# Two RWKV chunks in step, precedence for their short operations, and later rotary sums, in a two-layer hybrid block

## The chip, the cores and the metric

The kernel runs on one core of a Trainium2 chip. The metric is the device time of one execution in microseconds; the median of several runs is compared. The profile is of one further execution. TensorE, the engine of the matmuls, appears in it as PE, its weight loads as PEld; VectorE is DVE, ScalarE is ACT, GpSimd is POOL, and SyncE, which issues nearly all DMA transfers, is SP.

## The reference

Two layers over 256 context tokens and 1024 latent tokens of width 1024. Each layer normalises and modulates, projects once, and gives the columns to three groups of heads: gated linear attention (GLA), windowed softmax attention with rotary positions, and RWKV-7. Their outputs go through one output projection, and a SwiGLU feed-forward part follows. The change is about the RWKV group, whose recurrence is this one, in two directions, for 4 heads of 64:

```python
def step(S, inp):
    rt, wt, kt, vt, kkt, at = inp
    sa = jnp.einsum('bhvk,bhk->bhv', S, kkt)
    S = (S * wt[:, :, None, :] - sa[..., None] * (kkt * at)[:, :, None, :]
         + vt[..., None] * kt[:, :, None, :])
    return S, jnp.einsum('bhvk,bhk->bhv', S, rt)
```

and about the rotary positions of the latent queries and keys, `x1*cos - x2*sin` and `x1*sin + x2*cos`.

## The kernel before

A layer runs in stages: the RWKV input columns (`in_rwkv`), the *mixer stage* (`mixers`, line 771), the windowed attention together with the backward GLA states, GLA with the output projection, the feed-forward part. The change touches the mixer stage of both layers, the first norms of the kernel, and one cost.

**How work is ordered.** On TensorE the order is written out by hand. `Weave` (line 721) holds generators ("jobs"). A job issues matmuls, and with them the operations of other engines, then yields how many nanoseconds later its next matmuls are due, or a condition (`after`, on keys such as `("s", i)`, "scan i is done") that must be known first. `TE.t` is the planner's clock: each matmul adds a cost (lines 154 to 160). `run` picks the job that is due first, the lowest rank on a tie. Rank 9 is the *filler*, `dense()`: the projections of 12 columns of 128 for the two other groups (`in_rest`), matmul by matmul, and a thirteenth column after the scan. Whenever the filler had less than 1000 ns of the last 3400, it is picked (`SHARE`, lines 24 and 749). The RWKV jobs start 22 or 20 us of planned time after the filler (`LEAD`). On the other engines, SP's DMA queue included, a scheduler decides at compile time: among operations whose inputs it takes to be there it issues the one that was traced first, and each engine then runs its queue strictly in that order, waiting at the head where an input is late.

**RWKV in the mixer stage** (`rwkv_mixer`, line 1104). 1280 tokens are 20 chunks of 64; chunk i is taken for both directions and all heads at once, as 4 pairs `u`. To solve a chunk's triangular system a unit lower matrix is inverted by doubling. `prep_a` (line 1168) loads the chunk (`load`, two DMA issues of `AK`), makes the Gram product `LQ` (16 records `ps_g`, evicted and masked by DVE in `gram`), takes the 2x2 level from a copy `ld`, and does levels 2 and 3. `prep_b` (line 1193) loads `VU` and `Vbd` (six DMA issues), scales `Ke` on POOL, does level 4, the Gram product `MP`, level 5, a sixth level of 64x64 blocks (`ps_y6`, `ps_w6`, written into `XF`), and transposes `Ke` into `KT`. A `level` (line 1143) is a chain of four links: 16 matmuls of 32x32 into `ps_y`, ACT's copy to `y` (line 1148), 1000 ns later 16 matmuls into `ps_w`, DVE's predicated copy into `X` (line 1153) and its block transpose into `XT` (line 1154), 1200 ns later the next level. A float32 matmul shows as two records in the profile. `scan` (line 1248) carries the state `SBD` through the chunks: `R` from `MP`, `Vbd` and the state (evicted to `Rbd` by DVE and ACT), then `X` times `R`, `VU`/`U`, the state update `ps_s`, and the outputs. `finish` (line 1294) normalises the outputs of a token block with some two dozen short DVE operations. Ranks: scan 0, `prep_b` 1, `prep_a` 2, `finish` 3; `prep_a` may be three chunks ahead of the scan, `prep_b` two.

**Drains of the filler** (`drain`, line 611, rank -1). ACT copies a finished `ps_in` bank (two banks of tag d). For queries and keys of latent tokens the halves are exchanged by four DMA transfers into `t1`; DVE multiplies `t1` by the sine (line 643), POOL multiplies `y` by the cosine (line 644), DVE adds (line 645). `in_gla` (line 674, rank -2) makes GLA's decays for 256 tokens, each direction ending with transposes through `tokens_of`; its `ps_gl` and the transposes share one PSUM bank (tag x).

**The start** (lines 1710 to 1732): the squares and their sums of the three token groups (`norm.add`) are issued first, then the norms of the three groups (`start_in`), then the first columns.

Of the kernel before, what the change touches and what calls it, by code (L numbers as in the profile page):

```python
# [10 lines left out]
F32 = mybir.dt.float32  # L11
# [134 lines left out]
def block_kernel(ctx: ExitStack, tc: tile.TileContext, a):  # L146
# [3 lines left out]
    class Tensor:  # L150
# [3 lines left out]
        def matmul(self, out, lhsT, rhs, **kw):  # L154
            n, k, m = math.prod(rhs.shape[1:]), lhsT.shape[0], math.prod(lhsT.shape[1:])
            if rhs.dtype == F32:
                self.t += n * 1.06 if k <= 32 else max(130.0 if m <= 64 else 215.0, n * 1.67)
            else:
                self.t += n / 2.4
            return nc.tensor.matmul(out, lhsT, rhs, **kw)  # L160
# [5 lines left out]
    TE = Tensor()  # L166

# [435 lines left out]
    def in_rest(l, h, cols, wpool, pool, own, ypool, pp, spawn):  # L603
# [7 lines left out]
        def drain(nm, g0, n, ps):  # L611
# [13 lines left out]
            elif nm[:2] == "gg":  # L625
                j = int(nm[2])
                th = tmp("th")
                S.activation(th[:, :n], y[:, :n], AF.Tanh, scale=0.5)
                V.scalar_tensor_tensor(y[:, :n], th[:, :n], 1.0, y[:, :n], ALU.add, ALU.mult)
                V.tensor_scalar(y[:, :n], y[:, :n], hc(l, "glan"), None, ALU.mult)  # L630
                SY.dma_start(d_gg[:, j, g0:g0 + n], y[:, :n])
            elif nm == "sv":
                yield 1300
                tokens_of(aux, tmp, y, g0, n, d_sv)
            else:
                if g0 >= CTX:
                    r0 = g0 - CTX
                    rp = ypool.tile([P, 2, 512], F32, name="rope", bufs=1)
                    SY.dma_start(rp, a["rope"][:, :, r0:r0 + 512])
                    t1 = tmp("t1")  # L640
                    for r in range(0, P, 32):
                        SY.dma_start(t1[r:r + 32], y[r ^ 32:(r ^ 32) + 32])
                    V.tensor_tensor(t1, t1, rp[:, 1, :], ALU.mult)
                    G.tensor_tensor(y, y, rp[:, 0, :], ALU.mult)
                    V.tensor_tensor(y, y, t1, ALU.add)
                hl_ = [pool.tile([P, 512], F32R, name="qk_hl", tag="tmp", bufs=5) for _ in range(2)]
                S.copy(hl_[0][:, :n], y[:, :n])
                V.tensor_tensor(hl_[1][:, :n], y[:, :n], hl_[0][:, :n].bitcast(F32), ALU.subtract)
# [25 lines left out]
    def in_gla(l, t0, pool, own, pp, dw):  # L674
# [8 lines left out]
        for d in range(2):  # L683
# [21 lines left out]
            if not keys_only:  # L705
# [6 lines left out]
                      lambda name: pool.tile([P, 512], F32, name=name, tag="tmp", bufs=5), z, t0, n, d_gk[:, :, d, :])  # L712

# [390 lines left out]
    def rwkv_mixer(l, t_first, pool, fpool, pp, spawn):  # L1104
# [6 lines left out]
        lev = pool.tile([P, 5, 128], U8, name="lev")  # L1111
        for i in range(5):
# [3 lines left out]
            V.tensor_copy(lev[:, i, :], lf.rearrange("p d n -> p (d n)"))  # L1116
# [16 lines left out]
        def gram(AK, w_, dst):  # L1133
            ps = new([P, 4, P], "ps_g")
# [7 lines left out]

        def level(lv, LQ, X, XT):
            py = new([P, 4, 32], "ps_y")
            for u, rs, cs in blocks:
                TE.matmul(py[rs, u, :], LQ[rs, u, cs], XT[rs, u, :])
            y = pool.tile([P, 4, 32], F32, name="y", bufs=4)
            S.copy(y, py)
            yield 1000
            pz = new([P, 4, 32], "ps_w")  # L1150
            for u, rs, cs in blocks:
                TE.matmul(pz[rs, u, :], y[rs, u, :], X[rs, u, :])
            V.copy_predicated(f2(X), lev[:, lv - 1, :], f2(pz))
            V.transpose(f2(XT), f2(X))
            yield 1200
# [12 lines left out]
        def prep_a():  # L1168
            load(0)
            for i in range(NC):  # L1170
                yield after(("s", i - 3))
                b = batch[i]
                if i + 1 < NC:
                    load(i + 1)
                AK = b["AK"]
                X = pool.tile([P, 4, 32], F32, name="X", bufs=2)
                XT = pool.tile([P, 4, 32], F32, name="XT", bufs=2)
                G.tensor_copy(X, eye32.unsqueeze(1).to_broadcast([P, 4, 32]))
                LQ = pool.tile([P, 4, P], F32, name="LQ", bufs=3)
                gram(AK, 3, LQ)  # L1180

                ld = pool.tile([P, 4, 32], F32, name="ld")
                for r in range(0, 128, 32):
                    S.copy(ld[r:r + 32], LQ[r:r + 32, :, r % 64:r % 64 + 32])
                V.copy_predicated(f2(X), lev[:, 0, :], f2(ld))
                V.transpose(f2(XT), f2(X))
                yield 3400
                for lv in range(2, 4):
                    yield from level(lv, LQ, X, XT)
                b.update(LQ=LQ, X=X, XT=XT)  # L1190
                at["a", i] = TE.t + 900

        def prep_b():
            for i in range(NC):
                yield after(("a", i), ("s", i - 2))
                b = batch[i]
                cc, Dt, AK, LQ, X, XT = (b[n] for n in ("cc", "Dt", "AK", "LQ", "X", "XT"))
                VU = pool.tile([P, 512], F32, name="VU", bufs=3)
                vb = Vbd[i % 2]
                for d in range(2):  # L1200
                    c = cc[d]
                    src = d_v[c % 2 * 64:c % 2 * 64 + 64, c // 2, :]
                    SY.dma_start(VU[0:64, d * 256:(d + 1) * 256], src)
                    s4 = src.rearrange("s (q h n) -> s q h n", q=2, h=2)
                    for hp in range(2):
                        SY.dma_start(vb[H[hp], 2 * d:2 * d + 2, H[hp]], s4[:, :, hp, :])

                Ke = pool.tile([P, 4, P], F32, name="Ke")
                G.tensor_tensor(Ke, AK[:, :, 2:4, :].rearrange("p u w n -> p u (w n)"),
                                Dt.unsqueeze(2).to_broadcast([P, 4, P]), ALU.mult)  # L1210
                yield from level(4, LQ, X, XT)
                MP = pool.tile([P, 4, P], F32, name="MP", bufs=2)
                gram(AK, 2, MP)
                yield 0
                yield from level(5, LQ, X, XT)

                xf = XF[i % 2]
# [13 lines left out]
                KT = pool.tile([P, 4, P], F32, name="KT", bufs=2)  # L1231
# [11 lines left out]
                b.update(VU=VU, vb=vb, KT=KT, MP=MP, X=xf)  # L1243
                at["b", i] = TE.t + 900
# [3 lines left out]
        def scan():  # L1248
            for i in range(NC):
# [77 lines left out]
        for rank, gen in enumerate((scan(), prep_b(), prep_a(), finish_all())):  # L1327
            spawn(gen, rank, LEAD[l])
# [379 lines left out]
    with ExitStack() as e1:  # L1708
# [3 lines left out]
        with pool_of("x0", side="right") as xpool, pool_of("ad0", side="right") as apool, \  # L1712
# [198 lines left out]
```

## Time and profile before

| | us |
|---|---|
| median of 3 runs | 3771.24 |
| lowest and highest run | 3764.25, 3771.63 |
| the profiled execution | 3780.98 |
| its span, first to last instruction | 3779.2 |
| TensorE busy | 3598.1 (95%) |
| DVE, ACT, POOL busy | 2352.7, 1528.3, 692.3 |

A busy time is the union of an engine's instructions; matmuls overlap in the pipeline, so a busy TensorE isn't TensorE at its peak. The granted clock is a share of 2.4 GHz: 0.50 is the lower level, 1.2 GHz. "Idle before" an instruction is the time its engine stood still ahead of it, and the arrow names what ended that. "issue" is time for which the profile shows no wait.

### The profile page before, as it was taken

How to read it: one execution, taken by the hardware profiler on the slowest of the kernel's cores; microseconds unless marked ns; L12 is line 12 of the kernel's file. 1: busy time of each engine (PE TensorE's matmuls, PEld its weight loads, DVE VectorE, ACT ScalarE, POOL GpSimd, SP SyncE). 2: the span in 40 equal slices, each digit the busy share in tenths (PEclk: the TensorE clock that was granted, in tenths of full speed). 3: DMA queues.
4: the chain of work that ended last, by engine and by line, in shares of the span. 5: the costliest groups of instructions: out<-in, count | busy, mean ns of one | idle time of the engine just before them, and what ended most of it. 6: DMA issues, size and time to landing. Idle time of an engine off the chain costs nothing. (4 is left out here: it accounts for less than half of the span.)

```text
span 3779.2 us, 76437 instructions
## 1 busy us (share of the span) xinstructions
PE 3598.1 (95%) x30714; PEld 2823.4 (75%) x30714; DVE 2352.7 (62%) x4660; ACT 1528.3 (40%) x3170; POOL 692.3 (18%) x979
## 2 busy tenths in 40 slices
PE   7999999999999999999999998889999999999998
PEld 4767677656787888888888766667777778888787
DVE  4764545555567777756776783445566576666766
ACT  4444633345424333333442553543366243333213
POOL 3122222101234000000442232222211340000002
PEclk8999999999999999999999999989979999999999
DMA  5253342453231333325421234343321423221521
GB/s 181 104 171 107 110 126 85 116 162 92 88 109 63 113 112 106 116 70 196 134 91 57 86 146 124 112 122 112 87 81 35 129 101 97 77 89 62 195 67 62
DMA packets 310769, 405.79 MB, mean 107 GB/s; under 512 B 52880, under 2 KB 210192, under 8 KB 308368
## 3 DMA queue, kind: packets, MB, share of 16 engines
q1 hardware_dynamic: 310416, 400.92, 33.9%
q8 instruction: 242, 3.96, 0.4%
q14 instruction: 111, 0.91, 0.1%
HBM read 290.54 MB, written 105.03 MB: 105 GB/s over the span
## 5 line engine op out<-in xcount | busy, mean ns | idle before, releaser
L160 PE MATMUL ps_in<-h,w_hl 128*128 128x512 f32 (+1 forms) x2928 | 723.6, 387 | 12.3 <-ACT h L386 7.9
L160 PEld LDWEIGHTS ps_in<-h,w_hl 128*128 128x128 f32 x2928 | 491.0, 194 | 138.4 <-issue 50.1
L160 PE MATMUL ps_gu<-f,hl 128*128 128x512 f32 (+1 forms) x2400 | 568.6, 389 | 9.8 <-DVE hl L399 4.8
L160 PE MATMUL ps_d<-g,w_hl 128*128 128x512 f32 (+1 forms) x2688 | 557.4, 369 | 8.8 <-DVE x L1675 6.4
L160 PEld LDWEIGHTS ps_d<-g,w_hl 128*128 128x128 f32 x2688 | 463.8, 189 | 102.8 <-DVE x L1675 11.4
L160 PEld LDWEIGHTS ps_gu<-f,hl 128*128 128x128 f32 x2400 | 443.1, 190 | 105.2 <-DVE hl L399 5.7
L1675 DVE SCALAR_TENSOR_TENSOR x<-ps_d,mods,x 128x512 f32<-128x512 f32 (+1 forms) x448 | 291.0, 684 | 133.1 <-PE ps_d L160 132.4
L160 PE MATMUL ps_gu<-T,hl 128*128 128x512 f32 x1440 | 346.9, 390 | 1.5 <-DVE u L1576 1.5
L160 PEld LDWEIGHTS ps_gu<-T,hl 128*128 128x128 f32 x1440 | 268.8, 188 | 57.7 <-ACT g L398 1.9
L263 POOL TENSOR_TENSOR ada<-ada 128x256 f32<-128x256 f32 x112 | 90.5, 841 | 691.4 <-DMA x<-d_gt 560.0
L351 POOL TENSOR_TENSOR nacc<-nacc,nsq 128x512 f32<-128x512 f32 (+1 forms) x52 | 60.7, 1168 | 778.9 <-ACT nsq L350 776.2
L398 ACT CAST hl<-S 128x512 fp32r<-128x512 f32 x160 | 98.3, 621 | 252.4 <-PE ps_gu L160 159.1
L398 ACT CAST w_hl<-w_raw 128x1024 fp32r<-128x1024 f32 (+1 forms) x100 | 101.0, 1014 | 244.5 <-PE ps_d L160 194.1
L398 ACT CAST hl<-raw 128x512 fp32r<-128x512 f32 x156 | 96.6, 622 | 220.7 <-PE ps_gu L160 196.2
L1026 DVE TENSOR_REDUCE mx<-ps_ss 128x1 f32<-128x640 f32 (+2 forms) x144 | 107.5, 747 | 113.5 <-PE ps_ss L160 113.0
L160 PE MATMUL ps_o<-m,w_hl 128*128 128x512 f32 (+1 forms) x720 | 166.5, 381 | 0.0
L399 DVE TENSOR_TENSOR hl<-S,hl 128x512 fp32r<-128x512 f32 x160 | 109.9, 689 | 65.8 <-ACT hl L398 65.5
L160 PEld LDWEIGHTS ps_o<-m,w_hl 128*128 128x128 f32 x720 | 125.8, 191 | 32.5 <-issue 7.7
L399 DVE TENSOR_TENSOR w_hl<-w_raw,w_hl 128x1024 fp32r<-128x1024 f32 (+1 forms) x100 | 119.9, 1203 | 43.1 <-ACT w_hl L398 42.7
L399 DVE TENSOR_TENSOR pT<-ps_st,pT 128x512 fp32r<-128x512 f32 (+1 forms) x168 | 109.0, 657 | 33.8 <-ACT pT L398 33.4
L160 PEld LDWEIGHTS ps_x<-f,hl 128*128 128x128 f32 x960 | 124.5, 191 | 6.6 <-issue 0.8
L160 PE MATMUL ps_x<-f,hl 128*128 128x256 f32 x960 | 127.1, 283 | 0.0
(355 smaller groups left out, 6024.2 us busy)
## 6 DMA issues: line engine op xcount, KB each, us to landing
w_raw<-in_w_in_dram SPq DMA_DIRECT2D x44, 512.0 KB, 3.7
raw<-in_w_gate_dram SPq DMA_DIRECT2D x44, 512.0 KB, 3.7
raw<-in_w_up_dram SPq DMA_DIRECT2D x44, 512.0 KB, 3.5
x<-d_gt SPq DMA_DIRECT2D x88, 256.0 KB, 3.9
AK<-d_ab SPq DMA_DIRECT2D x80, 256.0 KB, 3.5
w_raw<-in_w_down_dram SPq DMA_DIRECT2D x40, 512.0 KB, 4.2
d_gt<-u SPq DMA_DIRECT2D x68, 256.0 KB, 2.0
d_ab<-W SPq DMA_DIRECT2D x16, 1024.0 KB, 4.2
```

The source lines that it names most:

```text
L160: return nc.tensor.matmul(out, lhsT, rhs, **kw)
L263: G.tensor_tensor(acc[:, s], acc[:, s], ps_[n % 2], ALU.add)
L351: (G if 0 < o < 5 else V).tensor_tensor(self.acc[g0], self.acc[g0], sq[:, :n], ALU.add)
L398: S.copy(dst[:, 0], src)
L399: V.tensor_tensor(dst[:, 1], src, dst[:, 0].bitcast(F32), ALU.subtract)
L1026: V.tensor_reduce(m_, psf[:, :nk * P], AX.X, ALU.max)
L1675: V.scalar_tensor_tensor(x[:, o, g0:g0 + n], ps[:, :n], mods[:, l, s, 40 + o:41 + o], x[:, o, g0:g0 + n], ALU.mult, ALU.add)
```

## The change

*Doublings in step.* `prep_a`, `prep_b` and `level` go. One job `prep` of rank 1 runs 21 iterations. Iteration i starts chunk i (the young one: load, `LQ`, 2x2 level) and ends chunk i - 1 (the old one: `VU`, `Vbd`, `Ke`, `MP` at the head of the iteration). Its two steps do levels 2 and 3 of the young chunk and levels 4 and 5 of the old one together: `X2` and `XT2` hold both chunks' matrices as two halves, one group of 32 matmuls fills `ps_y`, one copy of 256 columns evicts it, one group fills `ps_w`, one predicated copy and one transpose of 256 columns follow. The masks are laid out as `lev2` for either parity. The pauses stay 3400, 1000, 1200 and 300 ns. The sixth level, `XF` and `KT` follow for the old chunk.

*Precedence.* In `gram`, `prep` and `scan` the engines V, S and G are wrapped by `First`: each operation is traced under `tc.high_priority(600)`, that is, it counts for the scheduler as traced 600 instructions earlier. SP isn't wrapped.

*Rotary sums.* POOL's product with the cosine comes first and at once; the job then yields 3500 ns, and DVE's product with the sine is traced only then and pinned behind all that is traced on DVE up to that point (`keep_in_program_order`). The DVE sum and what follows are traced behind it.

*GLA.* Each direction of `in_gla` ends with a pause of 2000 ns.

*Planner's cost.* A float32 matmul with 64 rows and 64 columns of weights counts 0.9 ns a column.

*Start.* The squares and sums of the last token group are issued after the norms of the first two groups.

```diff
-                self.t += n * 1.06 if k <= 32 else max(130.0 if m <= 64 else 215.0, n * 1.67)
+                self.t += n * 1.06 if k <= 32 else n * 0.9 if k == m == 64 else max(130.0 if m <= 64 else 215.0, n * 1.67)
...
+    class First:
+        def __init__(self, engine):
+            self.engine = engine
+        def __getattr__(self, name):
+            def issue(*args, **kw):
+                with tc.high_priority(600):
+                    return getattr(self.engine, name)(*args, **kw)
+            return issue
+    FIRST = First(V), First(S), First(G)
...
-                    V.tensor_tensor(t1, t1, rp[:, 1, :], ALU.mult)
                     G.tensor_tensor(y, y, rp[:, 0, :], ALU.mult)
+                    yield 3500
+                    tc.keep_in_program_order(V.tensor_tensor(t1, t1, rp[:, 1, :], ALU.mult))
                     V.tensor_tensor(y, y, t1, ALU.add)
...
             tokens_of(lambda name: pp.tile([P, 512], F32, name=name, tag="x"),
                       lambda name: pool.tile([P, 512], F32, name=name, tag="tmp", bufs=5), z, t0, n, d_gk[:, :, d, :])
+            yield 2000
...
         def gram(AK, w_, dst):
+            V = FIRST[0]
...
+        X2 = pool.tile([P, 2, 4, 32], F32, name="X2")
+        XT2 = pool.tile([P, 2, 4, 32], F32, name="XT2")
...
-        def prep_a():
+        def prep():
+            V, S, G = FIRST
             load(0)
-            for i in range(NC):
+            for i in range(NC + 1):
                 yield after(("s", i - 3))
...
+                p = i % 2
+                young, old = batch[i] if i < NC else None, batch[i - 1] if i else None
+                hv = slice(0, 2) if i < NC and i else slice(p, p + 1) if old is None else slice(1 - p, 2 - p)
...
+                yield 3400 if young is not None else 0
+                both = [(h, b["LQ"]) for h, b in ((p, young), (1 - p, old)) if b is not None]
+                for step in range(2):
+                    py = new([P, 2, 4, 32], "ps_y")
+                    for h, LQ in both:
+                        for u, rs, cs in blocks:
+                            TE.matmul(py[rs, h, u, :], LQ[rs, u, cs], XT2[rs, h, u, :])
+                    y = pool.tile([P, 2, 4, 32], F32, name="y", bufs=2)
+                    S.copy(y[:, hv], py[:, hv])
+                    yield 1000
+                    pz = new([P, 2, 4, 32], "ps_w")
+                    for h, LQ in both:
+                        for u, rs, cs in blocks:
+                            TE.matmul(pz[rs, h, u, :], y[rs, h, u, :], X2[rs, h, u, :])
+                    V.copy_predicated(f3(X2[:, hv]), lev2[:, step, p, hv].rearrange("p h n -> p (h n)"), f3(pz[:, hv]))
+                    V.transpose(f3(XT2[:, hv]), f3(X2[:, hv]))
+                    yield 1200
...
         def scan():
+            V, S, G = FIRST
...
-        for rank, gen in enumerate((scan(), prep_b(), prep_a(), finish_all())):
+        for rank, gen in ((0, scan()), (1, prep()), (3, finish_all())):
...
-            for o in range(KD):
-                norm.add(o, *GROUPS[2])
             h = {}
-            for g0, n in GROUPS:
+            for i, (g0, n) in enumerate(GROUPS):
+                for o in range(KD if i == 2 else 0):
+                    norm.add(o, g0, n)
                 start_in(0, norm, act, h, g0, n)
```

## Rows read from the trace of the kernel before

**Rows 1.** the page of the profile: the whole execution
```profile
span 3779.2 us, 76437 instructions
```

**Rows 2.** windows of both mixer stretches: us, busy us by engine, clock, DMA
```profile
240.00:735.00 495.00, 457.68 (x8214) 357.01 (x8213) 237.16 (x741) 210.18 (x545) 115.65 (x208) 0.94 0.40 114
2262.00:2742.00 480.00, 431.01 (x8062) 330.04 (x8060) 229.68 (x684) 204.17 (x526) 118.31 (x211) 0.95 0.39 114
```

**Rows 3.** TensorE's waits, 240 to 735 us: who <- releaser: us, times, longest
```profile
PE ps_y L160 <- DVE XT L1154: 10.5, 11, 2.6
PE ps_g L160 <- DMA AK<-d_ab: 6.2, 1, 6.2
PE ps_gl L160 <- ACT vt L600: 4.3, 5, 1.7
PE ps_w L160 <- ACT y L1227: 3.5, 4, 1.4
```

**Rows 4.** TensorE's waits, 2275 to 2742 us
```profile
PE ps_r L160 <- ACT Rbd L1266: 12.6, 7, 4.3
PE ps_gl L160 <- ACT vt L600: 10.0, 5, 4.3
PE ps_y L160 <- DVE XT L1154: 8.0, 7, 4.2
PE ps_g L160 <- DMA AK<-d_ab: 6.5, 1, 6.5
```

**Rows 5.** timeline of 2505 to 2520 us: start, duration, instruction [idle before <-releaser]
```profile
2511.36 0.69 DVE L643 TENSOR_TENSOR t<-t,rope 128x512 f32<-128x512 f32 x1 [5.07 <-DMA t<-in]
2511.48 1.69 POOL L644 TENSOR_TENSOR in<-in,rope 128x512 f32<-128x512 f32 x1 [2.46 <-DMA t<-in]
...
2511.96 0.30 DVE L1153 COPY_PREDICATED X<-lev,ps_w 128x128 f32<-128x128 uint8 x1
...
2518.90 1.94 PE L160 MATMUL ps_r<-Rbd,XF 128*64 128x128 f32 x8 [4.31 <-ACT Rbd L1266]
```

**Rows 6.** windows of 4 us in layer 0's mixer stretch
```profile
344.00:348.00 4.00, 2.26 (x108) 1.94 (x109) 3.34 (x8) 3.41 (x6) 0.60 (x1) 0.99 0.30 66
348.00:352.00 4.00, 2.62 (x40) 2.15 (x40) 1.81 (x4) 1.45 (x5) 3.67 (x5) 0.50 0.60 201
```

**Rows 7.** windows of the tile ps_in alone, layer 1
```profile
2640.00:2660.00 20.00, 9.79 (x35) 1.00 0.42 124
2700.00:2720.00 20.00, 4.89 (x16) 1.00 0.20 56
```

**Rows 8.** timeline of 569 to 574 us: a lone group and a double one
```profile
569.40 0.34 PEld L160 LDWEIGHTS ps_y<-XT,LQ 32*32 32x32 f32 x32 [0.17 <-issue]
...
569.78 1.43 PE L160 MATMUL ps_in<-h,w_hl 128*128 128x512 f32 x5
...
573.05 0.34 PEld L160 LDWEIGHTS ps_w<-X,y 32*32 32x32 f32 x32 [0.17 <-issue]
...
573.80 0.73 PE L160 MATMUL ps_in<-h,w_hl 128*128 128x512 f32 x2
```

**Rows 9.** groups by line, whole execution: busy us, mean ns, idle before
```profile
L160 PE MATMUL ps_y<-XT,LQ 32*32 32x32 f32 x5760 | 88.0, 196 | 20.6 <-DVE XT L1154 18.5 <-issue 1.1 <-DVE rw_rs_y L424 0.9
...
L1154 DVE STREAM_TRANSPOSE XT<-X 128x128 f32<-128x128 f32 x160 | 49.2, 308 | 4.1
...
L1153 DVE COPY_PREDICATED X<-lev,ps_w 128x128 f32<-128x128 uint8 x160 | 47.2, 295 | 85.2 <-PE ps_w L160 84.4
...
L1148 ACT COPY y<-ps_y 128x128 f32<-128x128 f32 x160 | 42.2, 264 | 146.3 <-PE ps_y L160 144.3
...
L643 DVE TENSOR_TENSOR t<-t,rope 128x512 f32<-128x512 f32 x20 | 16.5, 826 | 31.3 <-DMA t<-in 31.3
```

**Rows 10.** timeline of 38 to 50 us, the start
```profile
47.31 2.07 DVE L399 TENSOR_TENSOR w_hl<-w_raw,w_hl 128x1024 fp32r<-128x1024 f32 x1 [6.27 <-ACT w_hl L398]
...
50.37 0.58 PE L160 MATMUL ps_in<-h,w_hl 128*128 128x256 f32 x1 [7.20 <-ACT h L386]
```

More of the change, by code (lines that the diff above doesn't have):

```diff
@@ L1110, in rwkv_mixer @@
         eye32 = load_const(pool, "eye32")
-        lev = pool.tile([P, 5, 128], U8, name="lev")
+        lev1 = pool.tile([P, 128], U8, name="lev1")
+        lev2 = pool.tile([P, 2, 2, 2, 128], U8, name="lev2")
         for i in range(5):
@@ L1115, in rwkv_mixer @@
             SY.dma_start(lf, a["cst"][:, o:o + 256].rearrange("p (d n) -> p d n", d=2)[:, :, 0:64])
-            V.tensor_copy(lev[:, i, :], lf.rearrange("p d n -> p (d n)"))
+            if i == 0:
+                V.tensor_copy(lev1, lf.rearrange("p d n -> p (d n)"))
+            for p in range(2) if i else ():
+                V.tensor_copy(lev2[:, (i - 1) % 2, p, p if i < 3 else 1 - p], lf.rearrange("p d n -> p (d n)"))
         SBD = pool.tile([P, 4, P], F32, name="SBD")
@@ L1141, in rwkv_mixer @@
         blocks = [(u, slice(r, r + 32), slice(r % 64, r % 64 + 32)) for u in range(4) for r in (0, 32, 64, 96)]
[L1143 to L1155, printed above, removed]
         def load(i):
@@ L1166, in load @@
             b.update(cc=cc, AK=AK, Dt=Dt)
-        def prep_a():
+        X2 = pool.tile([P, 2, 4, 32], F32, name="X2")
+        XT2 = pool.tile([P, 2, 4, 32], F32, name="XT2")
+        f3 = lambda ap: ap.rearrange("p h u n -> p (h u n)")
+        def prep():
+            V, S, G = FIRST
             load(0)
-            for i in range(NC):
+            for i in range(NC + 1):
                 yield after(("s", i - 3))
[L1172 to L1217, printed above, removed]
@@ new lines, in prep @@
+                p = i % 2
+                young, old = batch[i] if i < NC else None, batch[i - 1] if i else None
+                hv = slice(0, 2) if i < NC and i else slice(p, p + 1) if old is None else slice(1 - p, 2 - p)
+                if young is not None:
+                    if i + 1 < NC:
+                        load(i + 1)
+                    X, XT = X2[:, p], XT2[:, p]
+                    G.tensor_copy(X, eye32.unsqueeze(1).to_broadcast([P, 4, 32]))
+                    young["LQ"] = LQ = pool.tile([P, 4, P], F32, name="LQ", bufs=3)
+                    gram(young["AK"], 3, LQ)
+                    ld = pool.tile([P, 4, 32], F32, name="ld")
+                    for r in range(0, 128, 32):
+                        S.copy(ld[r:r + 32], LQ[r:r + 32, :, r % 64:r % 64 + 32])
+                    V.copy_predicated(f2(X), lev1, f2(ld))
+                    V.transpose(f2(XT), f2(X))
@@ new lines, in prep @@
+                if old is not None:
+                    cc, Dt, AK = (old[n] for n in ("cc", "Dt", "AK"))
+                    old["VU"] = VU = pool.tile([P, 512], F32, name="VU", bufs=3)
+                    old["vb"] = vb = Vbd[p]
+                    for d in range(2):
+                        c = cc[d]
+                        src = d_v[c % 2 * 64:c % 2 * 64 + 64, c // 2, :]
+                        SY.dma_start(VU[0:64, d * 256:(d + 1) * 256], src)
+                        s4 = src.rearrange("s (q h n) -> s q h n", q=2, h=2)
+                        for hp in range(2):
+                            SY.dma_start(vb[H[hp], 2 * d:2 * d + 2, H[hp]], s4[:, :, hp, :])
+                    Ke = pool.tile([P, 4, P], F32, name="Ke")
+                    G.tensor_tensor(Ke, AK[:, :, 2:4, :].rearrange("p u w n -> p u (w n)"),
+                                    Dt.unsqueeze(2).to_broadcast([P, 4, P]), ALU.mult)
+                    old["MP"] = MP = pool.tile([P, 4, P], F32, name="MP", bufs=2)
+                    gram(AK, 2, MP)
@@ L1218, in prep_b @@
+                if old is None:
+                    continue
+                X, XT, LQ, xf = X2[:, 1 - p], XT2[:, 1 - p], old["LQ"], XF[p]
                 for r in (0, 32, 64, 96):
@@ L1230, in prep_b @@
                     TE.transpose(pt[:, u, :], Ke[:, u, :], eye)
-                KT = pool.tile([P, 4, P], F32, name="KT", bufs=2)
+                old["KT"] = KT = pool.tile([P, 4, P], F32, name="KT", bufs=2)
                 S.copy(KT, pt)
@@ L1242, in prep_b @@
                             xf[ra:ra + 32, 2 * d:2 * d + 2, rb % 64:rb % 64 + 32], pz[ra:ra + 32])
-                b.update(VU=VU, vb=vb, KT=KT, MP=MP, X=xf)
-                at["b", i] = TE.t + 900
+                old["X"] = xf
+                at["b", i - 1] = TE.t + 900
         ow = fpool.tile([P, NT, 256], F32, name="ow")
         def scan():
+            V, S, G = FIRST
             for i in range(NC):
```

## The prediction

> **What bounds the kernel now.** First the page: the span of the profiled execution is 3779.2 us [rows 1], and TensorE is busy nearly all through it. Its 95% hides stages with different limits, so the next view is the windows over the two stretches that the change edits, the mixer stage of layer 0 (240 to 735 us) and of layer 1 (2262 to 2742 us) [rows 2]. TensorE is busy for 457.68 of 495 us and 431.01 of 480 us: 37.3 and 49.0 us of idle time, 86.3 in all. The mean granted clock there is 0.94 and 0.95, so some 0.06 x 495 = 30 and 0.05 x 480 = 24 us more go to the lower level of 1.2 GHz, part of it under the idle time. No engine other than TensorE is busy for half of either stretch. So TensorE's order of work sets the end, and what can be won is idle time, clock, and TensorE time lost between small groups of matmuls.
>
> Third, who releases TensorE in these stretches. In layer 0 the RWKV levels wait for the transposed block XT (10.5 us), for y (3.5 us), GLA's ps_gl for the copy that empties the one bank of tag x (4.3 us), and the first Gram product for its first load (6.2 us) [rows 3]. In layer 1 it is ACT's copy of Rbd (12.6 us), the same ps_gl (10.0), XT (8.0) and the first load (6.5) [rows 4]. XT, Rbd and y are copies of 0.2 to 0.4 us: the waits are queueing. The timeline round 2511 us shows one case [rows 5]: DVE stands 5.07 us on the rotary product of line 643, whose four transfers haven't landed; the predicated copy queued behind it starts 0.6 us after that product does, the Gram eviction, ld, X and Rbd follow, and TensorE idles 4.31 us. POOL stands 2.46 us on the same transfers.
>
> Fourth, the clock in short windows [rows 6]: with TensorE busy 2.26 of 4 us from 344 us the clock is still 0.99, and in the next 4 us it is 0.50. A wait is thus paid for again after it has ended.
>
> Fifth, the filler. Matmuls of ps_in take 9.79 of 20 us at 2640, but 4.89 of 20 at 2700 to 2720 [rows 7]: in layer 1 the dense columns are almost used up as the scan ends.
>
> **The change part by part.** *Two chunks in step.* The matmuls stay the same in number and shape. Per layer four levels of 20 chunks (80 copies y; 160 in both layers [rows 9]) become two steps of 21 iterations (42). Each has a group of ps_y and one of ps_w: 2 x 160 = 320 groups in both layers become 2 x 84 = 168, 152 fewer. What does a group cost beside its matmuls? A lone group (32 records) starts 0.17 us after PEld's previous load ended, and the filler starts 0.38 us after it does: 0.55. Two groups back to back hold 0.17 + 0.75 = 0.92 us [rows 8]. A merged pair looks like that second form, so one merge saves 1.10 - 0.92 = 0.18 us where both groups stood alone, and nothing where they stood together already, as the second form shows to happen. I take 0.1 us: 15 us, bounds 0 and 27.
>
> By the Trainium skill (TensorE: Matmul & The Clock Gate, "Part 3: Packing small matmuls"), a pack takes one matmul's duration and about 4 ns for each further tile. By it a merge would save one duration, 0.196 us in this trace [rows 9], and 152 of them 30 us, an estimate; but here a second group of 32 adds 0.37 us rather than 0.13 [rows 8], so the trace disagrees and the sum doesn't use it.
>
> The evictions double in width and halve in number. Copy y, predicated copy and transpose take 264, 295 and 308 ns at 128 columns [rows 9]; 256 columns aren't in the trace: between 1 and 2 times that. At twice, the chain per step is 0.87 us longer. The planned pauses (1000 and 1200 ns) don't grow, yet at most 528 ns must fit the first and 1206 the second, beside the drain of the matmuls; I count it as covered by the filler laid between the groups, and put what isn't into the debit below. MP's Gram product, Ke, VU and Vbd move to the head of the iteration. The eight DMA issues per chunk on SP stay eight. Vbd and XF are rewritten only after the scan that read them (the iteration waits for s(i-3)), so SP's queue gets no longer wait. What is late next is the chain: the levels of two chunks used to run as two generators, now one generator issues all of them in series.
>
> *Precedence.* 600 places for the short operations on DVE, ACT and POOL change which ready operation goes first, not their number. They pass finish's burst of some two dozen short DVE operations, drains and GLA's chain. It can't stop an operation that has started, or the head of a queue that waits for a transfer. Queued behind now are the copies of ps_in (two banks) and the tag-x copies.
>
> *Rotary product pinned, 3500 ns later.* The transfers of an x block are waited for on DVE for 31.3 us in all [rows 9]. The pin puts the product behind what was traced on DVE up to then, so the RWKV operations of the example run first. POOL's product isn't moved and still blocks POOL; behind it wait Ke, tmp, XF and X's unit block, with several us of slack each; I cost that at nothing, and at its observed 2.46 us per case if the slack is gone.
>
> *GLA's pause of 2000 ns* after the token transposes lets ACT empty the bank: 14.3 us of waits are in play [rows 3, 4]. The added pauses lengthen GLA's chain, not TensorE's.
>
> *Planner's cost* of a 64x64 product (115 instead of 214 ns for 128 columns) only moves places in the order, in the later GLA stage too (64 columns: 58 instead of 130); nothing, bounds -2 and +2.
>
> *Start.* Eight squares and sums of the last token group move behind the norms of the first two. Now DVE idles 6.27 us for w_hl, cast by ACT after squares, and TensorE 7.20 us [rows 10]. Up to 3.5 us of ACT's squares leave that path; they come back before the third group is needed. I take 2, bounds -2 and 3.5.
>
> **The sum.** Waits: of 86.3 us idle, the first loads (6.2 + 6.5) stay. Queueing of RWKV's own short operations is 10.5 + 3.5 + 12.6 + 8.0 = 34.6; I take 60%, 21, since precedence removes queueing but not the head of a queue. GLA's 14.3: 80%, 11. Of the other 24.7, a fifth: 5. Together 37 (bounds 12 and 62). Clock: 37 / 86.3 = 43% of the idle time goes, and with it the same part of 30 + 24 us: 23 (bounds 5 and 40). Merging 15, start 2. That is 77 us. Debit for filler used up early, copies that RWKV now overtakes, and POOL: 10 (bounds 0 and 35). Net 67 us. The profiled execution (3781.0 us with what lies round its span) becomes 3714 us; against the median of the runs, 3771.2, I predict 3704 us.
>
> **Rivals.** *The waits stay, the merge pays.* If the waits come from transfers and from the order in which the operations become ready, precedence moves little. For it: the 5.07 us case is a transfer, and POOL isn't pinned. Against it: GLA's waits and the pin don't hang on precedence. Merge 15, GLA 11, start 2, clock 5 = 33 less some 3 of debit: 3741 us.
>
> *Nothing is left:* each cost sits at its poor bound, 0 + 12 + 5 - 2 against a debit of 13; 3769 us.
>
> *Slower: one chain outlasts the filler.* The dense columns cover the pauses of the scan. With all levels in series on one generator, a chunk's chain (two Gram products, LQ and ld, two steps of four links, the sixth level) may be planned longer than now, so that more filler goes into each chunk and it runs out early; what is left of the scan then has bare pauses. For it: [rows 7], layer 1 is already at this edge. Against it: while this chain pauses, the scan of the chunk before and two thirds of the filler remain, and a chunk's TensorE work shrinks. Price: without filler TensorE loses its 9 us of cover in 20; about 5 us of pause in a chunk stay idle, and the clock falls as in [rows 6], another 5 us on the other half: 10 us a chunk. The 77 us are gone after 8 such chunks of 40; with 11, the time is 3771 - 77 + 110 = 3804 us.
>
> **How the numbers follow.** Forecast 0.62 (3665 to 3740), waits stay 0.18, nothing left 0.08, slower 0.12. The range reaches past the second rival to the third's time: 3660 to 3770 us leaves out the slower case and a small tail below. A measurement of this kernel tells some 0.2%, 7.5 us, from no change. Faster by more: 0.62 + 0.18 = 0.80; within: 0.08; slower: 0.12.
>
> **What would show it.** Right: 84 copies y at about 0.37 us; TensorE idle in the two stretches near 50 us in all; ps_gl out of the waits; DVE's wait on the rotary transfers well under 31 us; both stretches some 30 us shorter; fewer lower-clock stretches. Wrong: ps_in gone from the last chunks while ps_y and ps_w wait for y and XT (the chain); waits of ps_in or ps_tv for ACT's copies (precedence starves the filler); idle time gone but the stretches as long as before (the filler was merely slower); gains in the stretches that a later stage gives back.

## The result, and the profile after

The changed kernel took 3726.0 us, median of 4 runs (3721.3 to 3735.5), beside 3771.4 of the kernel before on the same chip: ratio 0.9883, 95% interval 0.9853 to 0.9912. A second series gave 0.9903 (0.9887 to 0.9918). So the change is worth some 37 to 45 us. The profiled execution of after, 3721.8 us, lies near the lower end of its runs, that of before, 3781.0, above the runs shown; the two profiles differ by 59 us, 14 more than the medians. So a busy time or a clock read from one profile carries some of this spread.

Most of it comes from the two stretches that the change edits. The best borders are landmarks, not fixed times: from the first `ps_gt` to the last `ps_in` of a layer's mixer stage. The windows view over these, for the kernel before (the lines of [rows 2] cut at the same landmarks), columns as there, with a line of sums:

```profile
245.90:735.10 489.20, 452.24 (x8190) 353.06 (x8190) 236.07 (x739) 209.14 (x543) 115.65 (x208) 0.94 0.39 112
2271.70:2741.70 470.00, 424.42 (x8034) 326.14 (x8034) 222.72 (x673) 200.39 (x519) 111.77 (x202) 0.95 0.39 111
sum 959.20, PE 876.66 PEld 679.20 DVE 458.79 ACT 409.53 POOL 227.43; mean PE 438.33 PEld 339.60 DVE 229.40 ACT 204.76 POOL 113.71
```

and for the changed kernel:

```profile
245.40:709.50 464.10, 423.51 (x8190) 338.57 (x8190) 233.06 (x667) 205.19 (x507) 119.05 (x209) 0.98 0.41 118
2242.40:2688.70 446.30, 406.21 (x8034) 323.57 (x8034) 218.09 (x601) 195.84 (x481) 112.72 (x202) 0.97 0.40 116
sum 910.40, PE 829.72 PEld 662.14 DVE 451.15 ACT 401.03 POOL 231.77; mean PE 414.86 PEld 331.07 DVE 225.57 ACT 200.51 POOL 115.89
```

The two stages are 48.8 us shorter with the same 8190 and 8034 records of TensorE. Idle time is the length less the busy time: 82.5 us before, 80.7 after. So TensorE waits as long in all as it did; its *busy* time fell, by 46.9 us. The granted clock rose from 0.94 and 0.95 to 0.98 and 0.97. Counted as the share below full clock times the length, that is 29 + 24 = 53 us before and 9 + 13 = 22 after; with clocks rounded to 0.01, each sum is good to some 5 us.

The groups by line of the whole execution (busy us, mean ns, idle before), after, with the pair of matmul groups that lock-step merges, the three evictions of 256 columns, the wait of the pinned product and POOL's:

```profile
L160 PE MATMUL ps_y<-XT,LQ 32*32 32x32 f32 x5760 | 75.3, 194 | 29.1 <-DVE XT L177 26.0 <-DVE rw_rs_t L442 1.8 <-DVE rw_rs_y L443 1.2
L160 PE MATMUL ps_w<-X,y 32*32 32x32 f32 x5760 | 75.2, 195 | 15.0 <-ACT y L177 13.8 <-issue 1.0
...
L177 DVE COPY_PREDICATED X<-lev,ps_w 128x256 f32<-128x256 uint8 x76 | 34.0, 447 | 62.7 <-PE ps_w L160 61.2 <-issue 0.3
L177 DVE STREAM_TRANSPOSE XT<-X 128x256 f32<-128x256 f32 x76 | 33.7, 444 | 2.1
L177 ACT COPY y<-ps_y 128x256 f32<-128x256 f32 x76 | 28.1, 370 | 61.9 <-PE ps_y L160 61.1
...
L660 DVE TENSOR_TENSOR t<-t,rope 128x512 f32<-128x512 f32 x20 | 19.8, 992 | 14.9 <-DMA t<-in 11.9 <-issue 2.9
L657 POOL TENSOR_TENSOR in<-in,rope 128x512 f32<-128x512 f32 x20 | 29.6, 1478 | 90.2 <-DMA t<-in 79.9 <-ACT y L177 7.3 <-issue 1.6
```

(Line 177 is the wrapper of precedence: all of RWKV's operations carry it.) `ps_y` had 88.0 us and waited 18.5 for `XT` [rows 9]; it has 75.3 and waits 26.0. `ps_w`, with this row in the kernel before, fell from 85.9 to 75.2, and its wait for `y` rose to 13.8:

```profile
L160 PE MATMUL ps_w<-X,y 32*32 32x32 f32 x5760 | 85.9, 197 | 10.6 <-ACT y L1227 4.8 <-ACT y L1148 3.1 <-issue 2.0
```

TensorE's waits in the two stages after, the lines that answer to [rows 3] and [rows 4] (us in all, times, longest):

```profile
PE ps_y L160 <- DVE XT L177: 13.9, 9, 3.2
PE ps_g L160 <- DMA AK<-d_ab: 6.0, 1, 6.0
PE ps_s L160 <- DVE VU L177: 4.9, 5, 1.0
PE ps_w L160 <- ACT y L177: 4.8, 10, 0.9
...
PE ps_y L160 <- DVE XT L177: 12.1, 8, 3.5
PE ps_w L160 <- ACT y L177: 9.0, 9, 2.4
PE ps_g L160 <- DMA AK<-d_ab: 6.7, 1, 6.7
PE ps_r L160 <- ACT Rbd L177: 4.1, 5, 1.5
...
PE ps_gl L160 <- ACT vt L614: 0.4, 1, 0.4
```

`ps_gl`, 14.3 us before, is down to 0.4, `Rbd` in layer 1 fell from 12.6 to 4.1, DVE's stand on the rotary transfers from 31.3 [rows 9] to 11.9. In their place `XT`, `y` and `VU` are waited for longer.

### The profile page after: what moved, and what is told of

The parts are those of the page before. It is cut to its first block, busy times and chain, and to the rows that moved or that the text cites. A ratio compares the mean times of both kernels' runs of the same rounds, so it can differ in the third digit from the quotient of the medians.

```text
span 3719.8 us, 76157 instructions
## 1 busy us (share of the span) xinstructions
PE 3548.3 (95%) x30714; PEld 2800.8 (75%) x30714; DVE 2347.6 (63%) x4516; ACT 1518.4 (41%) x3094; POOL 693.1 (19%) x979
## 5 line engine op out<-in xcount | busy, mean ns | idle before, releaser
L160 PE MATMUL ps_in<-h,w_hl 128*128 128x512 f32 (+1 forms) x2928 | 708.1, 382 | 9.3 <-ACT w_hl L412 2.7
```

## The experiments

Each kernel ran in 5 rounds against the kernel before on its chip; ratios are to that, with 95% intervals, and 0.1% is 3.8 us.

### Taking one part out of the changed kernel

The changed kernel once more, as the measure of this series:

> The changed kernel again, as the base of the three runs beside it. Both theories expect what was measured: about 3726 us, 0.988 of the kernel before.

Measured: 3735.3 us, 0.9903 (0.9887 to 0.9918). Its profile, of an execution of 3741.6 us, is a second reading of the same kernel, between the same landmarks:

```profile
sum 919.50, PE 838.16 PEld 668.10 DVE 450.67 ACT 401.63 POOL 232.58; mean PE 419.08 PEld 334.05 DVE 225.34 ACT 200.81 POOL 116.29
```

Idle time is 81.3 us beside 80.7, so that reading holds; busy time is 8.4 us longer, at clocks of 0.97 and 0.96. Outside the two stages the kernel takes 2820.2 us here and 2820.0 in the kernel before: by this profile the whole gain lies in the stages.

Without precedence:

```diff
-    FIRST = First(V), First(S), First(G)
+    FIRST = V, S, G
```

> The changed kernel without the precedence of 600 places; all else stays. Theory A: the gain is TensorE's own time (half as many groups of 32x32 matmuls), the clock that follows it, and GLA's pause; waits of RWKV for its short operations come from heads of queues that wait for something late, which precedence can't pass. Then the time rises by 0 to 10 us, to 3726 to 3736. Theory B: precedence carries the gain, since RWKV's operations pass the bursts of finish, drains and GLA. Then the time rises by 25 us or more, to 3750 and above, and TensorE's waits for XT and y grow by some 20 us.

Measured: 3732.5 us, 0.9897 (0.9879 to 0.9914): no difference. The stages' sums stay where they were:

```profile
sum 916.30, PE 832.21 PEld 662.70 DVE 452.09 ACT 401.20 POOL 233.13; mean PE 416.10 PEld 331.35 DVE 226.04 ACT 200.60 POOL 116.56
```

916.3 us with 84.1 idle. Precedence brings nothing here, and the traces show why: it changes next to nothing in the order of the queues. With the operations of each engine listed in order of start, by name and size, 4495 of DVE's 4516 stand in the same order with and without it, 3083 of ACT's 3094 and 974 of POOL's 979; in the two stages, 20 of 2663 stand elsewhere. A few places can matter: in the next run, without the pin, some 60 stand elsewhere, the 20 products among them. But those that precedence changes brought nothing. So this run doesn't show that another order is worth nothing; it shows that 600 places hardly made one. Precedence alone, put into the kernel before, wasn't run.

The rotary product at once, as before (DVE's product ahead of POOL's, no pause, no pin), all else changed:

```diff
+                    V.tensor_tensor(t1, t1, rp[:, 1, :], ALU.mult)
                     G.tensor_tensor(y, y, rp[:, 0, :], ALU.mult)
-                    yield 3500
-                    tc.keep_in_program_order(V.tensor_tensor(t1, t1, rp[:, 1, :], ALU.mult))
```

> The changed kernel with the rotary product on DVE traced at once again, ahead of POOL's, without pause and pin. DVE's wait at the head of its queue for the rotary transfers should come back from 11.9 to about 31 us. Theory A (heads of queues make the waits): TensorE's waits for XT, VU, Rbd and Ubd grow by 10 us or more and the time by 8 to 20 us, to 3734 to 3746. Rival: POOL waits for the same transfers and isn't pinned, so nothing changes: within 4 us of 3726.

Measured: 3756.7 us, 0.9955 (0.994 to 0.997). DVE's stand on the transfers came back to 31.6 us, as expected; the time rose by more than either theory gave.

GLA's pause taken out, all else changed:

```diff
-            yield 2000
```

> The changed kernel without GLA's pause of 2000 ns. Before the change TensorE waited 14.3 us for the copy that empties the bank of tag x. Theory A: these waits come back, with some clock, and the time rises by 10 to 18 us, to 3736 to 3744. Rival: the waits were laid over others, and the time stays within 4 us of 3726.

Measured: 3753.5 us, 0.9947 (0.9929 to 0.9966). `ps_gl` waits 10.1 us again, and here too the time lies above both ranges. Either removal costs about 20 us beside 3735.3, together as much as the whole change, which would leave nothing for lock-step. My reading at this point, that lock-step itself brings nothing, was the theory of the next series; it fell.

### Putting one part into the kernel before

Lock-step alone: the kernel before with `prep`, `X2`, `XT2` and `lev2` of the change (one job of 21 iterations, 256-column evictions); precedence, rotary order, GLA's pause, planner's cost and start as before.

```diff
...
-        for rank, gen in enumerate((scan(), prep_b(), prep_a(), finish_all())):
+        for rank, gen in ((0, scan()), (1, prep()), (3, finish_all())):
...
```

> The kernel before with two chunks in step alone: precedence, the later rotary product, GLA's pause, the new cost of a 64x64 product and the new order of the start are left as before. Theory A (the gain is the two pauses' and lock-step takes back as waits of a longer serial chain what it saves in groups of matmuls): 3760 to 3778 us beside 3772 of the kernel before; the matmuls of ps_y and ps_w take some 7 us less per layer, and TensorE waits as much longer for XT, y and VU. Theory B (lock-step brings its own 15 us or more, and the single undos of the earlier runs only overlapped): 3740 to 3757 us.

Measured: 3755.1 us, 0.9949 (0.9928 to 0.9971), in theory B's range. Theory A's began at 3760, and the interval reaches to 3763; what speaks against A is the profile, of an execution of 3740.4 us, 15 under the median of its runs. The windows over the stages, and its rows of `ps_w` and `ps_y`:

```profile
243.60:718.30 474.70, 426.73 (x8190) 340.34 (x8190) 232.08 (x667) 205.09 (x505) 116.39 (x208) 0.97 0.40 115
2252.20:2709.30 457.10, 412.87 (x8035) 324.11 (x8034) 218.20 (x601) 195.69 (x481) 113.91 (x202) 0.95 0.39 112
sum 931.80, PE 839.60 PEld 664.45 DVE 450.28 ACT 400.78 POOL 230.30; mean PE 419.80 PEld 332.22 DVE 225.14 ACT 200.39 POOL 115.15
```

```profile
L160 PE MATMUL ps_w<-X,y 32*32 32x32 f32 x5760 | 75.9, 196 | 8.9 <-ACT y L1226 5.3 <-ACT y L1248 2.1 <-issue 1.4
L160 PE MATMUL ps_y<-XT,LQ 32*32 32x32 f32 x5760 | 75.8, 196 | 28.6 <-DVE XT L1233 18.8 <-DVE XT L1200 4.8 <-DVE rw_rs_y L439 2.0
```

Beside before, busy time falls by 876.7 - 839.6 = 37.1 us, of which 173.9 - 151.7 = 22.2 lie in these two groups; idle time rises from 82.5 to 92.2. For the other 14.9 us the clock is at hand: its loss, counted as above, falls from 53 to 37 us. Lock-step makes TensorE's work shorter and its waits longer, but takes back far less than it saves, where theory A had as much.

Both pauses alone, put into the kernel before:

```diff
-                    V.tensor_tensor(t1, t1, rp[:, 1, :], ALU.mult)
                     G.tensor_tensor(y, y, rp[:, 0, :], ALU.mult)
+                    yield 3500
+                    tc.keep_in_program_order(V.tensor_tensor(t1, t1, rp[:, 1, :], ALU.mult))
...
+            yield 2000
```

> The kernel before with the two pauses alone: the rotary product pinned 3500 ns later on DVE, and GLA's 2000 ns. Theory A: they carry the gain, 3732 to 3742 us, as much as the whole change; DVE's wait on the rotary transfers falls from 31.3 to about 12 us and ps_gl goes out of the waits. Theory B (they work only with lock-step): 3750 to 3765 us.

Measured: 3753.2 us, 0.9952 (0.9934 to 0.997): as much as lock-step alone, some half of the change. Theory A falls here, and theory B's number came, though not its reason: the pauses work without lock-step.

```profile
sum 937.70, PE 867.13 PEld 670.04 DVE 459.15 ACT 410.43 POOL 224.50; mean PE 433.56 PEld 335.02 DVE 229.58 ACT 205.22 POOL 112.25
```

Here it is the idle time that falls: 70.6 us beside 82.5, and 9.5 us of busy time with it. The two halves add up, within the intervals: 0.51% by lock-step and 0.48% by the pauses beside 0.97 and 1.17% by the change (in these single profiles the stages are 27.4, 21.5 and 48.8 us shorter).

Each pause alone, in the kernel before (the first hunk of the diff above, then the second):

> The kernel before with the rotary product pinned 3500 ns later on DVE, and nothing else. If the two pauses clear two independent waits, the pin alone brings about half of the 20 us that the pair brought: 3760 to 3766 us beside 3773 of the kernel before. If either wait takes the other's place (as the changed kernel without one of them, 3753 and 3757 us, stood where lock-step alone stood, 3755), the pin alone brings less than 5 us: 3768 to 3776.

> The kernel before with GLA's pause of 2000 ns alone. Independent waits: some 10 us, 3760 to 3766 us. One wait takes the other's place: less than 5 us, 3768 to 3776; ps_gl gone from TensorE's waits, and the 31 us of DVE on the rotary transfers still there.

Measured: pin 3765.6 us, 0.9973 (0.9959 to 0.9987); pause 3759.6 us, 0.9966 (0.9949 to 0.9984). Each is worth some 10 us, and they add up to the pair's 18 within the intervals. In the kernel before they clear waits that are largely independent: with the pin alone `ps_gl` still waits 5.0 and 10.1 us in the two layers; with the pause alone DVE still stands 21.7 us on the transfers, though that is 9.6 less than before. On top of lock-step it is not so: lock-step alone stands at 0.9949, with the pause alone added (and the change's other parts) at 0.9955, with the pin alone at 0.9947, with both at 0.9903 or 0.9883. There a single one brings nothing that can be measured. TensorE's waits in layer 1 without the pin, and DVE's group of line 660 without the pause, show that each removal brings back, beside its own wait, part of the one that the other measure was to clear:

```profile
PE ps_y L160 <- DVE XT L177: 9.2, 8, 2.3
PE ps_gl L160 <- ACT vt L614: 8.9, 3, 6.2
PE ps_w L160 <- ACT y L177: 7.7, 9, 1.9
```

```profile
L660 DVE TENSOR_TENSOR t<-t,rope 128x512 f32<-128x512 f32 x20 | 18.1, 905 | 24.9 <-DMA t<-in 24.6
```

Without the pin, `ps_gl` waits 8.9 us although GLA pauses; without the pause, DVE stands 24.6 us on the transfers although the product is pinned. Why the one brings the other back wasn't taken apart.

### What the remaining waits are

POOL's rotary product behind the 3500 ns as well, pinned in POOL's queue:

```diff
-                    G.tensor_tensor(y, y, rp[:, 0, :], ALU.mult)
                     yield 3500
+                    tc.keep_in_program_order(G.tensor_tensor(y, y, rp[:, 0, :], ALU.mult))
                     tc.keep_in_program_order(V.tensor_tensor(t1, t1, rp[:, 1, :], ALU.mult))
```

> The changed kernel with POOL's rotary product also behind the 3500 ns pause and pinned in its queue. POOL stands 79.9 us on the rotary transfers in the changed kernel. If that blocks RWKV's copies behind it (Ke, xf, X), the time falls by 4 to 12 us; if their slack covers it, as the prediction had it, within 4 us of the changed kernel's 3726 to 3735.

Measured: 3740.5 us, 0.9916 (0.9893 to 0.9939). POOL's stand on the transfers fell from 79.9 to 30.0 us, and the time didn't fall (it lies 5 us above the range of the changed kernel, within the intervals): what POOL has queued behind the product has its slack, as the prediction costed it.

In the changed kernel a wait of 2.69 us for `XT` ends at 443.59 us. DVE's queue ahead of it (start, duration, instruction, idle before):

```profile
438.13 0.43 DVE L707 SCALAR_TENSOR_TENSOR gl_z<-gl_z,gl_u 128x256 f32<-128x256 f32 x1 [2.65 <-ACT gl_u L706]
438.60 0.69 DVE L710 TENSOR_TENSOR_SCAN gl_u<-cst,gl_z 128x256 f32<-128x256 f32 x1
...
440.81 1.22 DVE L660 TENSOR_TENSOR t<-t,rope 128x512 f32<-128x512 f32 x1
442.06 0.44 DVE L177 COPY_PREDICATED X<-lev,ps_w 128x256 f32<-128x256 uint8 x1
442.40 0.68 DVE L661 TENSOR_TENSOR in<-in,t 128x512 f32<-128x512 f32 x1
443.00 0.44 DVE L177 STREAM_TRANSPOSE XT<-X 128x256 f32<-128x256 f32 x1
```

DVE stands 2.65 us at the head of its queue for GLA's logarithm. On ACT a load of the function table lies ahead of that logarithm and another ahead of the exponential after it, in the groups by line of the changed kernel 20 each:

```profile
L706 ACT ACT_TABLE_LOAD x20 | 25.7, 1283 | 0.4
L713 ACT ACT_TABLE_LOAD x20 | 25.7, 1283 | 8.4 <-issue 7.9 <-DVE gl_u L712 0.3
```

The Trainium skill (ScalarE: Activation LUTs, "Table sets: the hidden batching unit") counts one load for a logarithm followed by an exponential, since one set holds both. Here each of these 20 pairs has two, 1283 ns each; the trace disagrees with that count.

The logarithm replaced by an exponential of the same size; this kernel computes other decays, and only prices what goes with the logarithm:

```diff
-            S.activation(u, u, AF.Ln, bias=1.0)
+            S.activation(u, u, AF.Exp, scale=-1.0)
```

> The changed kernel with the logarithm of GLA's decays replaced by an exponential of the same size, so that ACT never changes its table between the two (the decays are other numbers; nothing else is left out). If the remaining XT waits come from heads of queues that wait in GLA's chain for ACT's table loads of 1.28 us, forty of them go, DVE's 2.65 us stands on gl_u shrink below 1.5, XT waits fall from 26 us in both layers by a third or more, and the time falls by 8 to 20 us under the changed kernel's 3726 to 3735. If the chain itself is what is waited for (wider copies in series), within 5 us of the changed kernel.

Measured: 3698.3 us, 0.9813 (0.979 to 0.9836), 0.7 to 0.9% under the changed kernel, some 30 us and more than the 8 to 20 expected. All forty loads are gone. DVE's group of line 707 (43.8 us of idle time for ACT in the changed kernel), TensorE's `ps_y`, and the stages' sums:

```profile
L160 PE MATMUL ps_y<-XT,LQ 32*32 32x32 f32 x5760 | 75.6, 194 | 26.5 <-DVE XT L177 23.2 <-DVE rw_rs_t L442 1.8 <-DVE rw_rs_y L443 1.2
...
L707 DVE SCALAR_TENSOR_TENSOR gl_z<-gl_z,gl_u 128x256 f32<-128x256 f32 x20 | 9.7, 483 | 19.2 <-ACT gl_u L706 19.0
```

```profile
sum 884.90, PE 824.70 PEld 659.27 DVE 453.14 ACT 349.15 POOL 232.92; mean PE 412.35 PEld 329.64 DVE 226.57 ACT 174.58 POOL 116.46
```

Idle time falls to 60.2 us, 20.5 less than with the change. But `XT` waits, which were to fall by a third, fell only from 26.0 to 23.2 us; what went are the waits for `VU`, `Ubd`, `KT` and, in layer 1, `y`. So the stretch at 443 us isn't the rule for `XT`. What the run does price is the loads themselves: listed as above, every operation of TensorE, DVE, ACT and POOL stands in the same order as in the changed kernel, with the forty loads gone, and ACT is busy 51.9 us less in the stages (40 times 1.283 is 51.3). Beside the loads only the numbers in the decays differ.

The same loads halved, with the computation kept: both directions of a token block in one pass.

```diff
...
+        z2 = gi[:, 0:2]
+        u2, e2 = (own.tile([P, 2, n], F32, name="gl_" + nm) for nm in "ue")
+        ps = pp.tile([P, 512], F32, name="ps_gl", tag="x").rearrange("p (d n) -> p d n", d=2)
         for d in range(2):
-            ps = pp.tile([P, 512], F32, name="ps_gl", tag="x")[:, :n]
-            TE.matmul(ps, dw[0:32, d, :], gi[0:32, 0, :])
...
-            S.activation(u, u, AF.Ln, bias=1.0)
+        S.activation(f(u2), f(u2), AF.Ln, bias=1.0)
...
```

> The changed kernel with GLA's two directions of a token block done in one pass (one bank, one operation of 512 columns for each of Abs, Exp, Ln and the exponentials), which computes the same and needs 20 table loads in the mixers in place of 40. If the loads at the heads of ACT's and DVE's queues are the price that leaving out all forty showed (37 us under the changed kernel of the same day), half of them bring 10 to 20 us: 3715 to 3725 us. If that gain came from the other numbers in the decays, or from the single long stand after each load, which remains, 0 to 6 us: 3729 to 3740.

And with DVE's subtraction behind the logarithm pinned:

```diff
+        yield 3500
-        V.scalar_tensor_tensor(f(z2), f(z2), 0.0, f(u2), ALU.min, ALU.subtract)
+        tc.keep_in_program_order(V.scalar_tensor_tensor(f(z2), f(z2), 0.0, f(u2), ALU.min, ALU.subtract))
```

> As the one pass for both directions, and DVE's subtraction behind the logarithm pinned 3500 ns later, as the change did with the rotary product. If DVE's stand at the head of its queue is what RWKV's operations wait for, DVE's 44 us of idle time before that subtraction fall below 15 and the time comes 5 to 12 us under the one pass without the pin; if ACT's own time for the loads is, within 4 us of it.

Measured: 3735.1 us, 0.9901 (0.9881 to 0.9921), and 3727.6 us, 0.988 (0.9857 to 0.9903). Neither is told apart from the changed kernel. With the pin the time comes 7.5 us under the one pass without it, as the expectation had it for DVE's stand, but the intervals overlap, so that isn't shown. The one pass has half the loads, and DVE's stand on the logarithm fell to 24.1 us, with the pin to 9.7, as expected; the stages are 911.6 us long with the one pass (910.4 with the change). TensorE's waits in layer 1 with the one pass show new names:

```profile
PE ps_r L160 <- ACT Rbd L177: 7.9, 6, 2.1
...
PE ps_y L160 <- DVE XT L177: 5.1, 6, 1.9
PE ps_w L160 <- ACT y L177: 4.9, 6, 2.1
PE ps_y L160 <- DVE dD L720: 4.9, 1, 4.9
PE ps_tv L164 <- POOL gi L727: 4.1, 2, 2.3
```

`XT` fell from 12.1 to 5.1 us, and 4.9 for `dD`, 4.1 for `gi` and 3.8 more for `Rbd` took its place; in layer 0 it rose from 13.9 to 16.4. So half as many loads, in this form, bring nothing that can be measured, while about 30 us went with all of them at an unchanged order. The one pass changes more than the loads: its operations on ACT and on DVE behind the logarithm are twice as wide, and both directions come due together. Whether that takes back what the loads give stays open, and so does what the other numbers in the decays did to the 30 us. No run computes the same without a logarithm, and of the kernels that compute the same none beats the changed one by more than can be measured.

## Why the prediction was right and wrong

The forecast, 3704 us with a range of 3660 to 3770, lies 22 us under the measured 3726; the sign and the range hold. The net of the sum was -67 us and came as -45 (by the interval -33 to -55; -37 in the second series). That the range held is in part luck: its largest term came as next to nothing, and the gain came through the clock and the merging. Term by term:

*Waits, -37: the step that failed.* Idle time in the two stages fell by 1.9 us, not 37. The 21 us that precedence was to take from `XT`, `y` and `Rbd` are nil: taking precedence out changes nothing. My reason for it, "copies of 0.2 to 0.4 us: the waits are queueing", took all queueing for a matter of choice between ready operations, and took it for granted that 600 places would change that choice; in the two stages they move 20 operations of 2663. What another order would have brought stays open. The head of a late queue, which I had named as what precedence can't touch, moved when it was moved: the pin and the pause clear 11.9 us of idle time and 9.5 of busy time, as the kernel with the pauses alone shows. Of GLA's 14.3 us the 80% that I took went, and more: `ps_gl` has 0.4 left. By the end lock-step's longer waits had taken it all back.

*The debit, +10: too small, and the wrong one.* It was to hold filler used up early, overtaken copies and POOL. POOL cost nothing, as costed. What grew are waits in RWKV's own chain: lock-step alone adds 9.7 us of idle time, with `XT` from 18.5 to 23.6 us and `VU` from 3.9 to 11.4, while `Rbd` falls from 13.8 to 5.1 and `y` stays; in the changed kernel `XT` and `y` stand at 26.0 and 13.8. I had counted the wider copies as covered by the pauses. Each of the three evictions of a step is some 0.11 to 0.15 us longer, and a late one now holds two chunks back; that this makes the waits longer is my reading, since no run changed the width alone.

*Merging, -15 (bounds 0 to 27): right in kind, too small.* 152 groups fewer took 22.2 us out of `ps_y` and `ps_w`, 0.15 us a merge where I took 0.1. By the rule of packing that the prediction cited from the Trainium skill (TensorE: Matmul & The Clock Gate, "Part 3: Packing small matmuls") it would have been 30, an estimate; the measured number lies between the two.

*Clock, -23: near in size, wrong in its reason.* The loss went from 53 to 22 us, 31 less; by the second profile of the changed kernel to 32, 21 less. I had tied it to idle time, 43% of the one with 43% of the other. Idle time stayed, and the clock rose: with lock-step alone, idle time up, layer 0 stands at 0.97 beside 0.94. So the sum of the waits doesn't settle the clock: the two profiles of the changed kernel have the same idle time and differ by 10 us of it. What made the difference wasn't isolated.

*The pin and the pause* had no term of their own beside 11 and a part of 21; they are worth 18 us together, some half of the change. The planner's cost, put at nothing, wasn't run by itself.

*Start, -2: gone.* The first `ps_in` comes 5.1 us earlier (45.3 us beside 50.4, [rows 10]), the first `ps_bv` at 162.9 beside 163.4 us. The windows between the two, before and after:

```profile
50.37:163.40 113.03, 110.11 (x514) 85.56 (x515) 89.65 (x112) 60.17 (x101) 29.12 (x45) 0.95 0.22 76
```

```profile
45.32:162.90 117.58, 111.71 (x515) 86.05 (x516) 85.99 (x101) 59.81 (x98) 32.81 (x45) 0.94 0.20 73
```

The same matmuls take 4.6 us longer: idle time 5.9 us beside 2.9, busy time 1.6 more. What the norms of the first groups gained, waits for later weights and norms lose. The four kernels with the old start among the experiments reach the first `ps_bv` at 161.1 to 161.4 us, so nothing is left of this gain.

*What would show it.* 84 copies `y`, 76 of 256 columns at 370 ns: as forecast (0.37). `ps_gl` out of the waits, DVE's stand well under 31 us, fewer stretches at the lower clock: right. Stretches 30 us shorter each: 25.1 and 23.7. TensorE's idle time near 50 us: wrong, 80.7. Of the signs of failure two appeared in part. `ps_y` and `ps_w` wait longer for `XT` and `y`, with filler still there for all but the last chunk. And `ps_tv` waits 5.7 us for ACT's copies beside 1.6, but just as long without precedence, so it isn't precedence that starves the filler.

*The rivals.* "The waits stay, the merge pays", 3741 us, was nearer in its mechanism, and in its number too, 15 us off: precedence moved nothing, and what paid is the merge, GLA's pause and the pin. Its 5 us for the clock were too few. The slower rival didn't come, though its edge shows. In layer 1 of the changed kernel the last filler matmuls before the end of the scan, the next `ps_in` (the thirteenth column, when the scan is over), and the window between them:

```profile
2653.41 1.42 PE L160 MATMUL ps_in<-h,w_hl 128*128 128x512 f32 x5
...
2677.49 11.19 PE L160 MATMUL ps_in<-h,w_hl 128*128 128x512 f32 x48
```

```profile
2654.80:2677.50 22.70, 16.64 (x366) 13.98 (x365) 13.77 (x59) 9.13 (x26) 6.72 (x11) 1.00 0.18 53
```

For 22.7 us there is no filler, and TensorE stands idle for 6.1 of them, with the clock at 1.00. A chunk takes 446 / 20 = 22 us: one chunk has run short, where the rival needs eight, and it pays some 6 us, without the clock half of the price.

## What to carry to other kernels

Ask of each wait whether its releaser was late because something ready went ahead or because the head of its queue stood; a priority can help only the first, and a later place in the queue helped the second here. Then look whether the priority changed the order of the queues at all: here it hardly did. When small groups are merged, look at busy and idle time apart: here merging shortened the busy time while the waits in its chain grew, so that the change paid with as much idle time as before. And test parts both ways, out of the new kernel and into the old one: here the removals alone gave the whole gain to the two pauses, and only the additions showed that some half of it is lock-step's.

## What the runs showed of the hardware

Evictions of twice the width cost less than twice as much: ACT's copy 370 ns at 256 columns beside 264 at 128, DVE's predicated copy 447 beside 295, the block transpose 444 beside 308 ([rows 9] for the narrow ones).

A pair of logarithm and exponential in GLA's decays cost ACT two table loads of 1283 ns, all 20 times. With the forty loads gone and the order of all queues unchanged, the kernel was some 30 us shorter, though its decays were other numbers. DVE's product of line 643, 826 ns in the mean before, takes 992 in the changed kernel and 863 with the pauses alone; no run tells why.
